# A hybrid encoder layer on one core: first transfers reordered, products of ones ahead, and a row of scales broadcast by way of DRAM

## The chip, the core and the metric

The kernel runs on one core of one Trainium2 chip. The metric is the device time of one execution in microseconds (us): a median of 3 runs, 2376.36 us (2375.31 to 2376.83) before the change. The engines are PE (matrix products; PEld is its loading of the fixed operand), DVE, ACT and POOL (elementwise work), and SP, which here does nothing but issue transfers (DMAs). Each engine runs its own list of instructions strictly in the order in which they were written, and waits on semaphores for the others.

## What is computed

One encoder layer over two sequences: a prompt of 512 tokens and a sample of 1024 tokens, width 1024. Cut to what matters here:

```python
def rms_norm(x, w):
    return x * lax.rsqrt(jnp.mean(x * x, axis=-1, keepdims=True) + NORM_EPS) * w

def hybrid_layer(x, w_in, ...):
    h = rms_norm(x, n_pre_mix)
    proj = h @ w_in
    qkv_g, z_g, a_g, b_g, q_h, f_h, i_h, g_h, gate_raw = jnp.split(proj, IN_SPLITS, axis=-1)
    ...   # Gated DeltaNet over chunks, both directions: 4 heads
    ...   # HGRN2 over chunks, both directions: 4 heads, with values i_h
    merged = gates[:, :, 0] * y_a + gates[:, :, 1] * y_b
    x = x + rms_norm(merged @ w_out, n_post_mix)
    ff = (jax.nn.silu(h2 @ w_gate) * (h2 @ w_up)) @ w_down      # h2 = rms_norm(x, n_pre_ffn)
    return x + rms_norm(ff, n_post_ffn)
```

The scale of a token, rsqrt(mean(x * x) + eps), is called `rstd` below. It can be applied to `h` before a product or to the product's result.

## The kernel before

**Tiles.** Tokens are cut into blocks of 512 (`TB`): block 0 is the prompt, blocks 1 and 2 the sample. The activations lie transposed: a tile has 128 channels on its partitions and 512 tokens in its row, eight such tiles (`KD`) to a block. A float32 factor of a large product is split in two, `hi` (rounded to the fast format fp32r by an ACT copy) and `lo` (what DVE finds left over), and each product becomes three: hi·hi, hi·lo, lo·hi (`mm3`). Small products stay in plain float32, and a plain float32 product of 128 columns is two rows of the profile.

**The order.** `layer` does not issue instructions. It records them on a `Tape`; `Tape.schedule` then plays the record against a table of costs, engine by engine, gives tiles their buffers, and returns one order in which `Tape.emit` (the line L650 of the profile) writes all instructions. So nearly all rows have the line L650, and they are told apart by the memories that they touch: `la_a`, `ba_a`, `da_a` hold tiles of 512 and more, `sa_a` and `sm_a` constants and small tiles, `ha_a` the split activations, `wa_a` the split weights, `ra_a` a matrix of ones in fp32r, `bank` the eight banks of PSUM. The constants `HOLD`, `MSTEP`, `TOKENS`, `NORMED`, `NEAR` steer which work the record and the scheduler put forward: `HOLD` and `MSTEP` say which gate projections of the dense stream are kept back until the inverse of a DeltaNet head has come to a certain step.

**The start.** `prelude` begins with block 0. For each of the eight channel tiles k, SP loads a tile `xt` of the prompt and a tile `wv` of the weights `w_ih` (256 KB each). `values(k)` then splits both: ACT writes `hi[k]` = xt · gain (the gain is a column of `vec`, so it needs that small transfer too), DVE the rest `lo[k]`, ACT and DVE the same for the weights (`wh`, `wl`). PE adds twelve products of 128x512 to four banks (`pv`). That is 96 products for all k. Ahead of them in the record stand the constants (`ident`, `ones`, masks, the vector `vec`, and what `constants()` and `ab_constants()` work out of them).

**Scales.** Block 0 is projected without its scale; its `rstd` row is applied to the results (`pn` in `proj`) until normalised tiles are there. For blocks 1 and 2 (`rstd_row`, lines 1107 to 1130), four tiles of x are squared and summed on ACT, and a [128, 4] tile `y` of scales comes out, one token to a partition. The row that later work needs has all 512 scales on every partition. It is made with PE: for each of the four columns DVE writes a diagonal matrix `dg`, PE multiplies ones by it, and ACT copies the bank to `row`. `normed` (DVE) multiplies each `xt` of the sample by it.

**The inverse.** For each DeltaNet head, 32x32 triangles are written to DRAM (`u_sc`), read back in another layout (`iu`), inverted on POOL in 31 steps (`inverse`), written to DRAM (`w_sc`), and read as `wl`, of which DVE makes `wt`. PE multiplies by both.

Of the kernel before, what the change touches and what calls it, by code (L numbers as in the profile page):

```python
# [17 lines left out]
ALU = mybir.AluOpType  # L18
# [23 lines left out]
HOLD = ((2, 2, 1, 2), (2, 2, 2, 2))  # L42
MSTEP = (24, 28)
# [6 lines left out]
VSPLIT = 4  # L50
TRIG = 0
TOKENS, NORMED = 22.0, 30.0
# [4 lines left out]
class Op:  # L57

    __slots__ = ("idx", "eng", "meth", "args", "kw", "occ", "dur", "tiles", "need", "succ", "rel", "prio", "form", "unit",
# [104 lines left out]
class Tape:  # L164
# [10 lines left out]
    NEAR = 400  # L175
# [18 lines left out]
    def __init__(self, nc):  # L194
# [11 lines left out]
        self.shift = 0  # L206

# [5 lines left out]
    @contextmanager  # L213
    def sooner(self, n):

        self.shift += n
        yield
        self.shift -= n

# [138 lines left out]
    def add(self, eng, meth, args, kw):  # L358
# [3 lines left out]
        o.eng, o.meth, o.args, o.kw = eng, meth, args, kw  # L362
        o.form, o.unit, o.port, o.part = None, [o], 0, self.part
# [72 lines left out]
    def schedule(self):  # L436
# [4 lines left out]
        for o in ops:  # L441
            o.succ = []
            o.rel = 0.0
            o.asked = False
# [321 lines left out]
def layer(ctx, tc, x_p, x_s, w_out, n_post_mix, n_post_ffn, w_down, vec, xt_p, xt_s, w_in, w_br, w_gate, w_up,  # L766
# [121 lines left out]

    ident = ctile([P, P], "ident")
# [3 lines left out]
    nc.vector.memset(ones, 1.0)  # L893
    ones_r = nc.tile(rpool, [P, P], F32R, "ones_r")
# [15 lines left out]
    vcol = ctile([P, NVEC], "vcol")  # L910
    dma(vcol, vec)
# [27 lines left out]
    def px():  # L939
        return pl.tile(psx, [P, TB], F32, "px", "px", 5)  # L940
# [166 lines left out]
    def rstd_row(blk_):  # L1107
# [14 lines left out]
        pb = px()  # L1122
        for t in range(4):
            dg = sblk("dg")
            ts(dg, ident, y[:, t:t + 1], ALU.mult)
            mm(t4(pb)[:, t, :], ones, dg)
        row = blk("row")
        copy(row, pb)
# [3 lines left out]
    rstd = {}  # L1132
    waiting = []
# [21 lines left out]
    def prelude(q):  # L1155
# [9 lines left out]
        if q.si == 0:  # L1165
            xt = []
            hi, lo = h_tiles()
            pv = [px() for t in range(4)]
            wr = []
            for k in range(KD):  # L1170
                xt.append(load(0, k))
                wr.append(blk("wv"))
                dma(wr[k], w_ih[k])
# [19 lines left out]
            constants()  # L1193
            ab_constants()
# [6 lines left out]
            for k in range(KD):  # L1201
                act(sq[k], xt[k], AF.Square)
# [1455 lines left out]
```

## Time and profile before

| what | value |
|---|---|
| median of 3 runs | 2376.36 us |
| the profiled execution, its own time | 2376.19 us |
| its span, first to last instruction | 2374.5 us |
| time outside the span | 1.7 us |
| first product on PE | 7.55 us into the span |
| end of the last product on PE | 2367.2 us |
| products on PE (rows of the profile) | 14168 |

A page of the profile has busy times by engine, the chain of work that ended last (followed back from the end, at each step to what released it) and groups of equal instructions. The timeline lists instructions as start, duration, engine, line, operation, output <- input, form, count, and in brackets the idle time of the engine before them with what ended it. Rows of equal neighbours are merged: start of the first to end of the last. "SPq" is the issuing of a transfer on SP.

### The profile page before, as it was taken

The numbers are of one execution on the slowest core, as the hardware profiler recorded it, in microseconds if no ns is written. First come the engines' busy times: TensorE is split into PE (matmuls) and PEld (weight loads), VectorE is DVE, ScalarE is ACT, GpSimd is POOL, SyncE is SP. The second block draws the span as 40 slices with busy tenths as digits, with TensorE's granted clock in tenths as the row PEclk, the third lists the DMA queues.
The fourth block names the chain that finished last, engine by engine and source line by source line (L and its number), as shares of the span: only waits on it lengthen the run. The fifth ranks groups of instructions, "written<-read, shape, count | busy, mean of one in ns | idle before, by whom it ended". The sixth has DMA issues, their size and how long they took to land.

```text
span 2374.5 us, 37882 instructions
## 1 busy us (share of the span) xinstructions
PE 2359.3 (99%) x14168; PEld 1974.5 (83%) x14168; DVE 1722.2 (73%) x2826; ACT 1244.3 (52%) x2159; POOL 753.7 (32%) x1019
## 2 busy tenths in 40 slices
PE   8999999999999999999999999999999999999998
PEld 7888888888888888888888888888888888888887
DVE  6798789858848968759856885656787887544566
ACT  6766766746637647538442464545344444433343
POOL 0534524331602612502400011124676665200221
PEclk9999999999999999999999999999999999999999
DMA  6542343221320311325874463452455544674463
GB/s 224 173 134 87 123 134 92 94 81 45 108 77 23 112 67 54 100 75 173 281 258 157 159 212 118 152 173 77 167 192 177 178 159 173 217 244 138 148 205 128
DMA packets 194071, 337.72 MB, mean 142 GB/s; under 512 B 53248, under 2 KB 93024, under 8 KB 193888
## 3 DMA queue, kind: packets, MB, share of 16 engines
q1 hardware_dynamic: 193888, 335.31, 42.4%
q8 instruction: 111, 1.82, 0.3%
q14 instruction: 72, 0.59, 0.1%
HBM read 254.59 MB, written 80.66 MB: 141 GB/s over the span
## 4 chain that ended last, share of the span: by engine, by line
PE 98%; DVE 1%; ACT 0%; issue 0%; POOL 0%; DVEq 0%; POOLq 0%
PE bank L650 98%; DVE la_a L650 1%; DVE ba_a L650 0%; DVE wa_a L650 0%; ACT la_a L650 0%; ACT wa_a L650 0%; DVE da_a L650 0%; DVE sm_a L650 0%; POOL sm_a L650 0%; DVE sa_a L650 0%; POOL la_a L650 0%; ACT ba_a L650 0%; DVEq L2653 0%; ACT ha_a L650 0%; POOL sa_a L650 0%
## 5 line engine op out<-in xcount | busy, mean ns | idle before, releaser
L650 PE MATMUL bank<-ha_a,wa_a 128*128 128x512 f32 x5328 | 1278.7, 394 | 0.0
L650 PEld LDWEIGHTS bank<-ha_a,wa_a 128*128 128x128 f32 x5328 | 985.1, 188 | 196.5 <-issue 1.3
L650 PE MATMUL bank<-xr_a 128*128 128x512 f32 x1386 | 314.3, 389 | 0.0
L650 POOL TENSOR_TENSOR ba_a<-ba_a 128x512 f32<-128x512 f32 (+1 forms) x121 | 164.2, 1361 | 453.7 <-DVE sa_a L650 211.2
L650 PEld LDWEIGHTS bank<-xr_a 128*128 128x128 f32 x1386 | 260.3, 188 | 53.8
L650 PE MATMUL bank<-xr_a,ha_a 128*128 128x512 f32 x1200 | 275.3, 389 | 0.0
L650 PEld LDWEIGHTS bank<-xr_a,ha_a 128*128 128x128 f32 x1200 | 225.4, 188 | 46.6
L650 ACT ACTIVATE la_a<-la_a 128x512 f32<-128x512 f32 (+1 forms) x324 | 204.9, 647 | 56.8 <-DVE la_a L650 42.5
L650 DVE TENSOR_TENSOR wa_a<-ba_a,wa_a 128x1024 fp32r<-128x1024 f32 (+1 forms) x109 | 128.3, 1180 | 117.2 <-PE bank L650 76.4
L650 DVE TENSOR_TENSOR wa_a<-la_a,wa_a 128x1024 fp32r<-128x1024 f32 (+1 forms) x119 | 138.1, 1164 | 70.3 <-PE bank L650 41.0
L650 ACT ACTIVATE wa_a<-ba_a 128x1024 fp32r<-128x1024 f32 (+1 forms) x109 | 105.5, 969 | 154.3 <-PE bank L650 133.5
L650 ACT ACTIVATE wa_a<-la_a 128x1024 fp32r<-128x1024 f32 (+1 forms) x119 | 115.4, 974 | 127.8 <-PE bank L650 120.0
L650 ACT ACTIVATE ha_a<-ba_a 128x512 fp32r<-128x512 f32 (+1 forms) x124 | 79.7, 645 | 151.1 <-PE bank L650 115.3
L650 PE MATMUL bank<-wa_a,ha_a 128*128 128x512 f32 x624 | 144.2, 393 | 7.5 <-ACT wa_a L650 7.5
L650 DVE TENSOR_TENSOR la_a<-la_a 128x512 f32<-128x512 f32 (+2 forms) x200 | 138.4, 705 | 12.2 <-ACT la_a L650 11.5
L650 PEld LDWEIGHTS bank<-wa_a,ha_a 128*128 128x128 f32 x624 | 118.5, 190 | 32.2 <-ACT wa_a L650 7.5
L650 DVE TENSOR_TENSOR ha_a<-ba_a,ha_a 128x512 fp32r<-128x512 f32 (+1 forms) x124 | 125.9, 1021 | 13.9 <-ACT ha_a L650 13.7
L650 DVE TENSOR_TENSOR xr_a<-da_a,xr_a 128x1024 fp32r<-128x1024 f32 (+2 forms) x60 | 71.1, 1199 | 64.1 <-ACT xr_a L650 44.0
L650 POOL TENSOR_TENSOR la_a<-la_a 128x256 f32<-128x256 f32 (+1 forms) x63 | 62.8, 1011 | 172.2 <-DVE la_a L650 79.4
L650 ACT ACTIVATE xr_a<-da_a 128x1024 fp32r<-128x1024 f32 (+2 forms) x60 | 58.5, 987 | 106.2 <-PE bank L650 105.9
L650 PE MATMUL bank<-ha_a 128*128 128x512 f32 x480 | 112.1, 389 | 0.0
L650 PEld LDWEIGHTS bank<-ha_a 128*128 128x128 f32 x480 | 90.2, 188 | 18.6
(209 smaller groups left out, 3312.5 us busy)
## 6 DMA issues: line engine op xcount, KB each, us to landing
la_a<-lay_w_in SPq DMA_DIRECT2D x62, 512.0 KB
ba_a<-lay_w_in SPq DMA_DIRECT2D x38, 512.0 KB
ba_a<-lay_w_gate SPq DMA_DIRECT2D x35, 512.0 KB
ba_a<-lay_w_up SPq DMA_DIRECT2D x34, 512.0 KB
dram_a_sc<-xa_a SPq DMA_DIRECT2D x55, 256.0 KB
ba_a<-w_ffn_down SPq DMA_DIRECT2D x23, 512.0 KB
da_a<-dram_a_sc SPq DMA_DIRECT2D x22, 512.0 KB
ba_a<-dram_a_sc SPq DMA_DIRECT2D x20, 512.0 KB
```

The costliest lines, as they stand in the source:

```text
L650: f(*[m(a) for a in o.args], **{k: m(a) for k, a in o.kw.items()})
```

## The change

The first weight tile and the first tile of the prompt become the first two transfers of SP (`w0`, `x0`); `vec` is issued by ACT. Nine products of `ones` with itself open PE's list; nothing reads their result. For k = 0, the weights are split before the activations, the activations in two halves of 256 tokens, and the twelve products go in two groups of six, tokens 0 to 255 first. The constants and the squares of block 0 carry an earliest time in the scheduler's table (`later`, `LATER`). In `rstd_row`, the four diagonals, the four products and the copy give way to two transfers: `y` to DRAM (512 elements of 4 bytes), and from there one row of 2 KB to each of the 128 partitions. The steering constants get other values.

```diff
-HOLD = ((2, 2, 1, 2), (2, 2, 2, 2))
-MSTEP = (24, 28)
+HOLD = ((1, 2, 1, 1), (2, 2, 3, 2))
+MSTEP = (22, 26)
+LATER = 9000.0
-TOKENS, NORMED = 22.0, 30.0
+TOKENS, NORMED = 14, 50
...
-    NEAR = 400
+    NEAR = 250
...
+    @contextmanager
+    def later(self, t):
+
+        old, self.after = self.after, t
+        yield
+        self.after = old
...
+        o.after = self.after
...
-            o.rel = 0.0
+            o.rel = o.after
...
+    w0 = pl.tile(tp, [P, TB + 4], F32, "wv", "t", TBUFS)[:, 0:TB]
+    dma(w0, w_ih[0])
+    vcol = ctile([P, NVEC], "vcol")
+    dma(vcol, vec, nc.scalar)
+    x0 = pl.tile(gp, [P, TB], F32, "xt", "xt", 8)
+    halves = [slice(z * 2 * P, (z + 1) * 2 * P) for z in range(2)]
+    dma(x0, xt_p[0:P, 0:TB])
...
+    warm = pl.tile(psx, [P, TB], F32, "px", "px", 5)
+    for t in range(9):
+        mm(warm[:, 0:P], ones, ones)
...
-    vcol = ctile([P, NVEC], "vcol")
-    dma(vcol, vec)
...
-        pb = px()
-        for t in range(4):
-            dg = sblk("dg")
-            ts(dg, ident, y[:, t:t + 1], ALU.mult)
-            mm(t4(pb)[:, t, :], ones, dg)
+        sc = r_sc[blk_ - 1]
+        dma(sc.rearrange("t p -> p t"), y)
         row = blk("row")
-        copy(row, pb)
+        dma(row, bass.AP(tensor=sc.tensor, offset=sc.offset, ap=[[0, P], [1, TB]]))
         rstd[blk_] = row
...
             def values(k):
-                act(hi[:, k, :], xt[k], AF.Copy, scale=g_mix[:, k:k + 1])
                 hl = pl.tile(wsp, [P, 1024], F32R, "whl", "whl", 6)
                 wh, wl = hl[:, 0:TB], hl[:, TB:2 * TB]
-                split(wh, wl, wr[k])
-                stt(lo[:, k, :], xt[k], g_mix[:, k:k + 1], hi[:, k, :].bitcast(F32), ALU.mult, ALU.subtract)
-                for x, w in ((hi, wh), (hi, wl), (lo, wh)):
-                    for t in range(4):
-                        mm(pv[t], x[:, k, t * P:(t + 1) * P], w, k == 0 and w is wh and x is hi, k == KD - 1 and x is lo)
+                if k == 0:
+                    split(wh, wl, wr[k])
+                for z in halves if k == 0 else [slice(0, TB)]:
+                    act(hi[:, k, z], xt[k][:, z], AF.Copy, scale=g_mix[:, k:k + 1])
+                if k:
+                    split(wh, wl, wr[k])
+                for z in halves if k == 0 else [slice(0, TB)]:
+                    stt(lo[:, k, z], xt[k][:, z], g_mix[:, k:k + 1], hi[:, k, z].bitcast(F32), ALU.mult, ALU.subtract)
+                for ts_ in ((0, 1), (2, 3)) if k == 0 else (range(4),):
+                    for x, w in ((hi, wh), (hi, wl), (lo, wh)):
+                        for t in ts_:
+                            mm(pv[t], x[:, k, t * P:(t + 1) * P], w, k == 0 and w is wh and x is hi, k == KD - 1 and x is lo)
...
-            constants()
-            ab_constants()
+            with nc.later(LATER):
+                constants()
+                ab_constants()
...
-            for k in range(KD):
-                act(sq[k], xt[k], AF.Square)
+            with nc.later(LATER):
+                for k in range(KD):
+                    act(sq[k], xt[k], AF.Square)
```

What this does to the lists of the engines is shown at three places. A row is a line of the kernel, an operation, output <- inputs and the output's shape; the kernel after has other line numbers (L660 for L650). Equal neighbours are merged.

The first is the start of ACT's list, before: the table load, small constants from `ident` and `vec`, then `hi` of k = 0 (ha_a), a square (la_a), the weights (wa_a).

```order
L768 ACT_TABLE_LOAD
L650 ACTIVATE sm_a,sa_a<-sa_a 128x16
L650 ACTIVATE sm_a,sa_a<-sa_a 128x32
L650 ACTIVATE sa_a<-sa_a 128x1
L650 ACTIVATE sa_a<-sa_a 128x8
L650 ACTIVATE ha_a<-la_a,sa_a 128x512
L650 ACTIVATE la_a<-la_a 128x512
L650 ACTIVATE wa_a<-la_a 128x512
```

The same place after the change:

```order
L778 ACT_TABLE_LOAD
L660 DMA sa_a<-lay_vec 128x88
L660 ACTIVATE wa_a<-la_a 128x512
L660 ACTIVATE ha_a<-la_a,sa_a 128x256 x2
L660 ACTIVATE ha_a<-la_a,sa_a 128x512
L660 ACTIVATE wa_a<-la_a 128x512
L660 ACTIVATE ha_a<-la_a,sa_a 128x512
L660 ACTIVATE wa_a<-la_a 128x512
L660 ACTIVATE sa_a<-sa_a 128x1
```

The four small constants and the square stood ahead of the first weights; now the transfer of `vec` does, and the constants come after three pairs of splits.

The second place is the start of PE's list, before: banks 87 to 90 in turn, the four token groups of `pv`.

```order
L650 MATMUL bank_87<-wa_a,ha_a 128x512
L650 MATMUL bank_88<-wa_a,ha_a 128x512
L650 MATMUL bank_89<-wa_a,ha_a 128x512
L650 MATMUL bank_90<-wa_a,ha_a 128x512
L650 MATMUL bank_87<-wa_a,ha_a 128x512
```

And after, with `pv` in banks 88 to 91:

```order
L660 MATMUL bank_87<-sm_a 128x128 x9
L660 MATMUL bank_88<-wa_a,ha_a 128x512
L660 MATMUL bank_89<-wa_a,ha_a 128x512
L660 MATMUL bank_88<-wa_a,ha_a 128x512
L660 MATMUL bank_89<-wa_a,ha_a 128x512
L660 MATMUL bank_88<-wa_a,ha_a 128x512
L660 MATMUL bank_89<-wa_a,ha_a 128x512
L660 MATMUL bank_90<-wa_a,ha_a 128x512
```

Nine products of ones stand ahead, and the first six real ones need only the first half of the tokens.

The third place is SP's list where the sample's `xt` tiles and the first head's triangles pass, before:

```order
L650 DMA la_a<-lay_xt_sample 128x512 x5
L650 DMA ba_a<-lay_xt_sample 128x512 x3
L650 DMA dram_u_sc_116<-la_a 32x4x32 x8
L650 DMA ba_a<-dram_u_sc_116 32x1024 x4
L650 DMA ba_a<-lay_w_in 128x1024
```

And after, with the two transfers of the scales of block 1 (`r_sc`):

```order
L660 DMA la_a<-lay_xt_sample 128x512 x4
L660 DMA la_a<-lay_w_in 128x1024
L660 DMA la_a<-lay_xt_sample 128x512 x4
L660 DMA dram_r_sc_106<-sm_a 128x4x1
L660 DMA ba_a<-dram_r_sc_106 128x512
L660 DMA dram_u_sc_122<-la_a 32x4x32 x4
L660 DMA dram_u_sc_122<-ba_a 32x4x32 x4
L660 DMA ba_a<-dram_u_sc_122 32x1024 x4
```

The two transfers stand ahead of the eight stores of the triangles. Counted over the whole lists, PE has 11,839 products and transposes before and 11,840 after (nine more, eight fewer), DVE has four instructions fewer and ACT one ACTIVATE or COPY fewer. PE's list changes from 128x512 products to another shape and back 243 times before and 237 times after. The last 3,474 products and transposes of PE, from about 1580 us on, stand in the same order in both.

More of the change, by code (lines that the diff above doesn't have):

```diff
@@ L57 @@
 class Op:
-    __slots__ = ("idx", "eng", "meth", "args", "kw", "occ", "dur", "tiles", "need", "succ", "rel", "prio", "form", "unit",
+    __slots__ = ("idx", "eng", "meth", "args", "kw", "occ", "dur", "tiles", "need", "succ", "rel", "after", "prio", "form", "unit",
                  "asked", "port", "part")
@@ L206, in __init__ @@
         self.shift = 0
+        self.after = 0.0
     def apart(self, pairs=False):
@@ L1132, in layer @@
     rstd = {}
+    r_sc = [dram.tile([4, P], F32, name="r_sc%d" % i) for i in range(2)]
     waiting = []
@@ L1165, in prelude @@
         if q.si == 0:
-            xt = []
+            xt = [x0]
             hi, lo = h_tiles()
             pv = [px() for t in range(4)]
-            wr = []
+            wr = [w0]
             for k in range(KD):
-                xt.append(load(0, k))
-                wr.append(blk("wv"))
-                dma(wr[k], w_ih[k])
+                if k:
+                    xt.append(load(0, k))
+                    wr.append(blk("wv"))
+                    dma(wr[k], w_ih[k])
                 if k in AHEAD:
@@ L1180, in values @@
             def values(k):
-                act(hi[:, k, :], xt[k], AF.Copy, scale=g_mix[:, k:k + 1])
                 hl = pl.tile(wsp, [P, 1024], F32R, "whl", "whl", 6)
                 wh, wl = hl[:, 0:TB], hl[:, TB:2 * TB]
-                split(wh, wl, wr[k])
-                stt(lo[:, k, :], xt[k], g_mix[:, k:k + 1], hi[:, k, :].bitcast(F32), ALU.mult, ALU.subtract)
-                for x, w in ((hi, wh), (hi, wl), (lo, wh)):
-                    for t in range(4):
-                        mm(pv[t], x[:, k, t * P:(t + 1) * P], w, k == 0 and w is wh and x is hi, k == KD - 1 and x is lo)
+                if k == 0:
+                    split(wh, wl, wr[k])
+                for z in halves if k == 0 else [slice(0, TB)]:
+                    act(hi[:, k, z], xt[k][:, z], AF.Copy, scale=g_mix[:, k:k + 1])
+                if k:
+                    split(wh, wl, wr[k])
[5 more added lines that the diff above has]
+                            mm(pv[t], x[:, k, t * P:(t + 1) * P], w, k == 0 and w is wh and x is hi, k == KD - 1 and x is lo)
             for k in range(VSPLIT):
```

## The prediction

> **What bounds the kernel now.** First the page: busy time by engine, and the chain that ended last.
>
> ```profile
> PE 2359.3 (99%) x14168; PEld 1974.5 (83%) x14168; DVE 1722.2 (73%) x2826; ACT 1244.3 (52%) x2159; POOL 753.7 (32%) x1019
> PE 98%; DVE 1%; ACT 0%; issue 0%; POOL 0%; DVEq 0%; POOLq 0%
> ```
>
> PE is 99% busy and 98% of the chain. A busy PE need not be a fast one, so I asked for its waits next: all of them, over the whole span.
>
> ```profile
> PE bank L650 <- ACT wa_a L650: 7.5, 1, 7.5
> PE bank L650 <- DVE wa_a L650: 0.2, 1, 0.2
> ```
>
> PE waits 7.5 us once, for the first split weights, and 0.2 us later. From then on the time is the sum of PE's products and of what lies behind the last one. So three things can shorten it: an earlier first product, faster products, fewer products. The chain in order of time shows what the first product waits for:
>
> ```profile
> 5.21 0.32 DVE sm_a L650 x2
> ...
> 7.55 145.17 PE bank L650 x941
> ```
>
> Not a transfer: the chain comes from DVE's masks. The timeline shows what lies between, and the transfers.
>
> ```profile
> 0.80 1.28 ACT L768 ACT_TABLE_LOAD   x1 [0.80 <-PEq L2648]
> 0.80 0.39 SPq L650 DMA_DIRECT2D sa_a<-lay_vec  x1
> 0.90 0.17 DVE L650 MEMSET sm_a<- 128x128 f32 x1 [0.90 <-PEq L2648]
> 1.24 0.42 SPq L650 DMA_DIRECT2D la_a<-lay_xt_prompt  x1
> 1.71 0.43 SPq L650 DMA_DIRECT2D la_a<-lay_w_ih  x1
> 2.09 0.21 ACT L650 ACTIVATE sm_a<-sa_a 128x16 f32<-128x16 f32 x1
> 2.65 0.43 SPq L650 DMA_DIRECT2D la_a<-lay_w_ih  x1
> 2.72 0.20 ACT L650 ACTIVATE sa_a<-sa_a 128x1 f32<-128x1 f32 x1
> 5.63 0.21 ACT L650 ACTIVATE sa_a<-sa_a 128x8 f32<-128x8 f32 x1 [2.71 <-DVE sa_a L650]
> 5.75 0.71 ACT L650 ACTIVATE ha_a<-la_a,sa_a 128x512 fp32r<-128x512 f32 x1
> 6.36 0.61 ACT L650 ACTIVATE la_a<-la_a 128x512 f32<-128x512 f32 x1
> 6.88 0.61 ACT L650 ACTIVATE wa_a<-la_a 128x512 fp32r<-128x512 f32 x1
> 7.32 0.33 SPq L650 DMA_DIRECT2D la_a<-lay_w_ih  x1
> ```
>
> ACT stands idle for 2.71 us behind DVE; then `hi`, a square and the weights follow in a row, and PE starts.
>
> **Term 1, the first product.** When are `w0` and `x0` there? The transfer view of two windows, 0 to 4.0 us and 0 to 4.8 us:
>
> ```profile
> DMA packets 384, 0.50 MB, mean 125 GB/s; under 512 B 161, under 2 KB 161, under 8 KB 384
> DMA packets 518, 0.75 MB, mean 155 GB/s; under 512 B 176, under 2 KB 176, under 8 KB 518
> ```
>
> 0.50 MB had moved at 4.0 us and 0.75 MB at 4.8 us. `vec` and the first two tiles are 0.57 MB, so the pair was through at about 4.2 us, and at the latest near 4.8. Without `vec` ahead of it the pair's second is issued 0.47 us earlier (1.24 for 1.71): both there between 3.75 and 4.35 us, the first of them some 0.65 us (256 KB at that pace) before. I take 3.7 for `w0` and 4.35 for `x0`. ACT splits `w0` in 0.61 us, to 4.3. `vec` is the open piece: ACT issues it, behind its table load in the list. It goes out at 0.80 if the load doesn't hold the list up, at 2.08 if it does; before, it was read at 2.72, at most 1.92 us after its issue. That makes 2.7 to 4.0 us, in time either way; I take the later. At the worst it takes what the fifth tile took, issued at 2.65, whose landing let the thirteenth transfer go at 7.32 (the transfers use eight semaphores in turn): 4.7 us, so 6.8. Half of `hi` is 0.71 us less half of what 512 more columns cost in this row:
>
> ```profile
> 41.92 1.07 ACT L650 ACTIVATE wa_a<-la_a 128x1024 fp32r<-128x1024 f32 x1 [0.45 <-PE bank L650]
> ```
>
> (1.07 - 0.61) / 2 = 0.23, so 0.48 us. PE starts at 4.35 + 0.48 + 0.06 (the step from 7.49 to 7.55 above) = **4.9 us** instead of 7.55: **-2.65 us**, bounds 4.3 and 7.3. After that k = 1 needs the fifth tile's counterpart, issued 0.47 us earlier and so there at 6.85, split by 7.5; k = 0 keeps PE until 4.9 + 12 x 0.227 = 7.6. No wait there. The constants and squares that are moved behind cost ACT and DVE the same time later; these rows show the cover:
>
> ```profile
> 10.00:20.00 10.00, 10.00 (x42) 8.20 (x41) 6.39 (x11) 10.00 (x18) 0.14 (x2) 1.00 1.03 399
> 20.00:30.00 10.00, 10.00 (x46) 8.29 (x45) 4.32 (x5) 3.10 (x4) 0.00 (x0) 1.00 1.03 415
> ```
>
> (busy PE, PEld, DVE, ACT, POOL, then clock and transfers). ACT is full from 10 to 20 us and then idle for two thirds. In 23 us, from 3.7 to 26.7, it has 8 x (0.71 + 0.61 + 0.61) and four weight splits of 1.07, 20 us: it fits, with 3 us to spare. Without the cover each k would wait some tenths. A page of the Trainium skill speaks against this term: "ScalarE: Activation LUTs", What ACT_TABLE_LOAD costs, has 2.66 us for a load with its drain. By that `vec` would go out at 3.46, land at 5.4, and PE start at 5.9, 1.0 us later than I say. The trace disagrees: ACT's next instruction ran at 2.09, right behind the 1.28 us of the load.
>
> **Term 2, the pace of the first products.** The same products in two stretches, and the granted clock (the 1.00 before the last two numbers) in the first of them; last the group that most products are in (count, busy us, mean ns of one):
>
> ```profile
> 7.55 4.77 PE L650 MATMUL bank<-wa_a,ha_a 128*128 128x512 f32 x11 [7.55 <-ACT wa_a L650]
> 7.55 24.04 PE L650 MATMUL bank<-wa_a,ha_a 128*128 128x512 f32 x96 [7.55 <-ACT wa_a L650]
> 8.00:9.00 1.00, 1.00 (x4) 1.00 1.01 375
> L650 PE MATMUL bank<-ha_a,wa_a 128*128 128x512 f32 x5328 | 1278.7, 394 | 0.0
> ```
>
> The other 85 took 24.04 - 4.77 = 19.27 us, 0.227 each. The eleven took about 0.42 each, though the clock column says 1.00: PE begins at half pace, for some 4.2 us. That costs 11 x 0.227 = 2.5 us against 4.6 (4.77 less the 0.16 by which a product's row, 0.39, outlasts its step): 2.1 us. After the change `ones` is there at 1.07 (DVE's first row above), the nine products start at about 1.1, and PE is busy until 4.9 if they run at half pace: 2 rows x 0.111 (below) x 0.42 / 0.227 = 0.41 each, 3.7 in all. If what frees the pace is 4.2 us of busy time, it comes at 5.3, and one real product pays 0.2. So **-1.9 us**, bounds 0 and -2.1. "TensorE: Matmul & The Clock Gate", Part 1, in the Trainium skill has a rule by which it could be less: the pace doubles after a busy window of 3.4 us that runs free of the kernel, so 3.4 to 6.8 us of work may pass. By that the real products would run slow until 4.5 to 7.9 us and the term would be -2.1 to -0.6; the 4.2 us here lie inside.
>
> **Term 3, the products that go.** The four products of block 1 in PE's list, and what comes before and after:
>
> ```profile
> 77.08 0.17 DVE L650 TENSOR_TENSOR sm_a<-sm_a 128x4 f32<-128x4 f32 x1
> 77.28 0.87 DVE L650 TENSOR_SCALAR sm_a<-sa_a,sm_a 128x128 f32<-128x128 f32 x4
> 89.00 1.06 PE L650 MATMUL bank<-sm_a 128*128 128x128 f32 x8
> 89.81 1.41 PE L650 MATMUL bank<-ha_a,wa_a 128*128 128x512 f32 x5
> 106.92 2.10 DVE L650 SCALAR_TENSOR_TENSOR la_a<-la_a,sa_a 128x512 f32<-128x512 f32 x3
> ```
>
> Eight rows in 0.8 to 0.9 us, 0.111 each. Two blocks: 16 x 0.111 = **-1.8 us**. In their place SP writes and reads 512 numbers: the scale is there at 77.25 and first used at 106.92, almost 30 us later. The slowest stand-in, the eight stores and the read further down, takes 10.2 us from the first store to POOL's use (71.08 to 81.25), so PE doesn't see it; without the cover it would cost up to that. DVE's and ACT's part (0.87 and a copy per block) lay beside PE and gives nothing. The order has six changes of shape fewer; a return to 128x512 costs (1.41 - 0.39 - 4 x 0.227) = 0.11 us and the last small product before it 0.08 less, so 0.2 us in all: left out.
>
> **Sum.** 2.65 + 1.9 + 1.8 = 6.35 us off the execution's own 2376.19 (span 2374.5 plus 1.7): **2369.8**. The median of the runs shown is 0.17 above that execution, which I neglect.
>
> **Rivals.** (A) The products of ones free nothing, or late, and the real ones run at half pace as before: up to 2369.8 + 1.9 = 2371.7. For it: the clock column shows nothing of what holds the pace down. The Trainium skill's free window would end between 2369.6 and 2371.1. Chance 0.10. (B) `vec` is late, held up by more of ACT's list than the 1.28 us or between SP's big tiles, and PE starts between 5.9 and 7.3: 2370.8 to 2372.2. The Trainium skill's drain is the mild end of it. Against: it landed within 1.92 us before. 0.08. (C) The new order waits more. Before, PE waited 0.2 us after the start, but with DVE near full:
>
> ```profile
> 100.00:150.00 50.00, 50.00 (x405) 40.72 (x404) 44.90 (x92) 31.97 (x54) 24.01 (x50) 1.00 0.33 101
> 150.00:200.00 50.00, 49.90 (x380) 42.32 (x379) 46.66 (x82) 40.45 (x75) 29.00 (x58) 1.00 0.36 130
> ```
>
> DVE is idle for 8.4 of these 100 us (44.90 and 46.66 busy). Three more `pn` evictions come in, eight diagonals go, about even; but a block done early only gains what DVE can follow. If half of terms 1 and 2 is lost there or in small waits, 2372 to 2374.5. 0.15. (D) Slower: SP stands still. The read of the scales waits for the store's 512 pieces of 4 bytes, and behind it in SP's list are the stores of the first head's triangles, behind those POOL's inverse, behind that PE.
>
> ```profile
> 71.08 4.16 SPq L650 DMA_DIRECT2D dram_u_sc<-la_a  x8
> 76.58 1.98 SPq L650 DMA_DIRECT2D ba_a<-dram_u_sc  x4
> 81.25 0.42 POOL L650 TENSOR_TENSOR sm_a<-la_a,ba_a 128x31 f32<-128x31 f32 x1 [23.36 <-DMA ba_a<-dram_u_sc]
> 126.98 0.21 PE L650 MATMUL bank<-ba_a,la_a 32*32 32x32 f32 x1
> ```
>
> PE's first use of the inverse is its 588th product before; in the new order 620 real ones come ahead of it, some 33 x 0.227 = 7.5 us of work more. It decides from a hold-up of 7.5 us on. The eight stores, 1024 pieces, took 5.5 us to the read, so I expect 2 to 5. To be slower than 2381 it would take 7.5 + 6.35 + 4.75 = 18.6 us: price 5 us and more over before, time about 2382. 0.05. And the rest, 0.02, better than the bounds of the three terms.
>
> **How the numbers follow.** 0.2% is 4.75 us, about what can be told from no change here: faster means under 2371.6, slower over 2381.1. Forecast 0.60 (2368 to 2371.5), A 0.10, B 0.08, C 0.15, D 0.05, rest 0.02. Faster: 0.60, the rest, half of A and B: 0.71. Slower: D, 0.05. Same: 0.24. The range goes from 2367.8 (PE at 4.3, no slow product, six cheaper changes) to 2373.8, which takes in A, B and most of C.
>
> **What would show it.** Right: the 96 products of `pv` begin near 4.9 us, at 0.227 from the first or second on, and end near 26.8 instead of 31.6; PE's list of waits has one of under 1 us after that; DVE's first use of the scale lies well behind the read. Wrong: a wait of PE for `ha_a` at the start (B), products of 0.42 after 5.5 us (A), new waits for DVE's tiles between 40 and 200 us (C), or for `wl`'s (D).

## The result, and the profile after

| kernel | median | runs | ratio to before (95%) |
|---|---|---|---|
| before | 2376.77 us | 11 | 1 |
| after | 2382.78 us | 11 | 1.0026 [1.0017, 1.0035] |

The change makes the kernel slower by 0.26%, 6.2 us of 2376.4; faster by 6.6 us was forecast, in a range that ends at 2373.8. The profiled execution after took 2383.97 us. First its page: busy time by engine, and the chain by engine.

```profile
PE 2365.3 (99%) x14170; PEld 1976.6 (83%) x14170; DVE 1727.2 (73%) x2822; ACT 1246.9 (52%) x2158; POOL 757.3 (32%) x1019
PE 90%; DVE 5%; DMA 2%; ACT 1%; issue 1%; POOL 0%; SPq 0%; DVEq 0%; POOLq 0%; ACTq 0%
```

PE reads 99% busy as before, yet it is 90% of the chain instead of 98%, and transfers are 2% of it. PE's busy time even rose by 6.0 us; the products of ones are 3.9 of them, and yet it has fewer real products than before, so some of these ran longer. So next PE's waits, then the start of the timeline.

```profile
PE bank L660 <- DVE ba_a L660: 3.3, 3, 1.9
PE bank L660 <- DVE wa_a L660: 1.6, 3, 1.2
PE bank L660 <- issue: 1.2, 1, 1.2
PE bank L660 <- DVE sm_a L660: 1.1, 1, 1.1
PE bank L660 <- ACT wa_a L660: 1.1, 2, 0.6
PE bank L660 <- DVE la_a L660: 1.0, 1, 1.0
```

```profile
0.83 0.39 ACTq L660 DMA_DIRECT2D sa_a<-lay_vec  x1
1.12 3.93 PE L660 MATMUL bank<-sm_a 128*128 128x128 f32 x18 [1.12 <-DVE sm_a L660]
3.81 0.63 ACT L660 ACTIVATE wa_a<-la_a 128x512 fp32r<-128x512 f32 x1 [1.73 <-DMA la_a<-lay_w_ih]
4.51 1.52 ACT L660 ACTIVATE ha_a<-la_a,sa_a 128x256 fp32r<-128x256 f32 x3
5.07 22.06 PE L660 MATMUL bank<-wa_a,ha_a 128*128 128x512 f32 x96
```

The start came out as worked out: `w0` read at 3.81 (3.7 forecast), `x0` at 4.51 (4.35), the first real product at 5.07 (4.9), and 96 products in 22.06 us, 0.228 each from the first on. They end at 27.1 instead of 31.6, 4.5 us earlier. The list of waits has what that was lost to: apart from the 1.1 us for `ones`, about 8 us of new ones, 7 of them for results of DVE and ACT. What comes late there, the chain in order of time tells (pieces between 60 and 140 us):

```profile
66.51 8.24 DMA dram_r_sc<-sm_a
74.77 5.04 DMA ba_a<-dram_r_sc
...
84.00 3.83 DMA ba_a<-x_sample
...
95.71 0.70 DVE ba_a L660
...
96.46 2.58 PE bank L660 x8
...
102.78 8.40 DMA dram_r_sc<-sm_a
```

and SP's part of the timeline what stood behind it:

```profile
66.51 0.38 SPq L660 DMA_DIRECT2D dram_r_sc<-sm_a  x1
74.77 0.33 SPq L660 DMA_DIRECT2D ba_a<-dram_r_sc  x1
75.20 1.81 SPq L660 DMA_DIRECT2D dram_u_sc<-la_a  x4
...
82.25 1.71 SPq L660 DMA_DIRECT2D ba_a<-dram_u_sc  x4
84.00 0.42 SPq L660 DMA_DIRECT2D ba_a<-x_sample  x1
```

The store of 512 pieces of 4 bytes lands 8.2 us after its issue. SP stands before the read until then, and all behind it is late: the triangles, and a tile of `x_sample`. ACT squares that tile, is late with what follows in its list, DVE with it, and PE waits 1.9 us at 94.6. There is a second price. The view by windows shows busy time by engine, the granted clock (the number before the last two), then transfers:

```profile
95.00:96.00 1.00, 0.00 (x0) 0.00 (x0) 0.29 (x1) 1.00 (x3) 0.77 (x4) 1.00 0.99 395
96.00:97.00 1.00, 0.54 (x5) 0.54 (x5) 0.40 (x1) 1.00 (x2) 0.87 (x2) 0.89 0.84 330
97.00:98.00 1.00, 1.00 (x5) 0.81 (x4) 0.65 (x1) 1.00 (x3) 0.81 (x3) 0.50 0.51 186
98.00:99.00 1.00, 1.00 (x4) 0.81 (x3) 0.41 (x2) 0.28 (x2) 0.76 (x4) 0.50 0.62 125
99.00:100.00 1.00, 1.00 (x4) 0.81 (x3) 1.00 (x2) 0.94 (x1) 1.00 (x1) 0.50 0.99 375
100.00:101.00 1.00, 1.00 (x5) 0.78 (x5) 0.19 (x1) 1.00 (x4) 0.80 (x3) 0.90 0.27 107
```

Behind the wait the clock is halved for 3.4 us (0.11, three times 0.50 and 0.10 short of full, over 0.50), and PE counts as fully busy meanwhile. That costs up to 1.7 us and stands in no list of waits. It happens twice more, near 138 and 319 us (0.79 in the mean of 134 to 142, 0.76 of 316 to 323). Together this is an account of the loss, as an estimate: 8.2 us of new waits and three times 1.7 us of pace, less the 4.5 us of the start and 1.2 to 1.8 us for the products that went, make 7.0 to 7.6 us; the two profiled executions differ by 7.8 (2383.97 and 2376.19).

### The profile page after: what moved, and what is told of

Same layout as the page of the kernel before. It is cut to its first block, busy times and chain, and to the rows that moved or that the text cites. A ratio compares the mean times of both kernels' runs of the same rounds, so it can differ in the third digit from the quotient of the medians.

```text
span 2382.2 us, 37911 instructions
## 1 busy us (share of the span) xinstructions
PE 2365.3 (99%) x14170; PEld 1976.6 (83%) x14170; DVE 1727.2 (73%) x2822; ACT 1246.9 (52%) x2158; POOL 757.3 (32%) x1019
## 4 chain that ended last, share of the span: by engine, by line
PE 90%; DVE 5%; DMA 2%; ACT 1%; issue 1%; POOL 0%; SPq 0%; DVEq 0%; POOLq 0%; ACTq 0%
PE bank L660 90%; DVE la_a L660 3%; DVE ba_a L660 1%; DMA dram_r_sc<-sm_a 1%; ACT la_a L660 1%; DMA ba_a<-x_sample 1%; DVE wa_a L660 0%; DMA la_a<-lay_w_in 0%; DVE sm_a L660 0%; ACT ba_a L660 0%; SPq L660 0%; ACT wa_a L660 0%; POOL la_a L660 0%; DMA ba_a<-dram_r_sc 0%; DMA dram_g_sc<-la_a 0%
## 5 line engine op out<-in xcount | busy, mean ns | idle before, releaser
L660 PE MATMUL bank<-ha_a,wa_a 128*128 128x512 f32 x5328 | 1283.7, 395 | 2.1 <-DVE wa_a L660 1.6
L660 PEld LDWEIGHTS bank<-ha_a,wa_a 128*128 128x128 f32 x5328 | 986.9, 189 | 201.4 <-DVE wa_a L660 2.8
L660 PE MATMUL bank<-xr_a 128*128 128x512 f32 x1386 | 314.3, 389 | 0.0
L660 PEld LDWEIGHTS bank<-xr_a 128*128 128x128 f32 x1386 | 260.1, 188 | 54.0
L660 POOL TENSOR_TENSOR ba_a<-ba_a 128x512 f32<-128x512 f32 (+1 forms) x135 | 184.6, 1372 | 287.3 <-DVE ba_a L660 85.9
L660 PE MATMUL bank<-xr_a,ha_a 128*128 128x512 f32 x1200 | 275.2, 389 | 0.0
L660 PEld LDWEIGHTS bank<-xr_a,ha_a 128*128 128x128 f32 x1200 | 225.2, 188 | 46.8
L660 ACT ACTIVATE la_a<-la_a 128x512 f32<-128x512 f32 (+1 forms) x298 | 188.3, 649 | 52.1 <-DVE la_a L660 28.7
L660 DVE TENSOR_TENSOR wa_a<-ba_a,wa_a 128x1024 fp32r<-128x1024 f32 (+1 forms) x113 | 132.5, 1174 | 108.3 <-PE bank L660 54.6
L660 ACT ACTIVATE wa_a<-ba_a 128x1024 fp32r<-128x1024 f32 (+1 forms) x113 | 109.3, 968 | 164.5 <-PE bank L660 157.5
L660 DVE TENSOR_TENSOR wa_a<-la_a,wa_a 128x1024 fp32r<-128x1024 f32 (+1 forms) x115 | 134.0, 1166 | 55.7 <-PE bank L660 40.8
L660 ACT ACTIVATE wa_a<-la_a 128x1024 fp32r<-128x1024 f32 (+1 forms) x115 | 112.0, 976 | 108.9 <-PE bank L660 90.4
L660 ACT ACTIVATE ha_a<-ba_a 128x512 fp32r<-128x512 f32 (+1 forms) x126 | 80.4, 645 | 153.6 <-PE bank L660 114.3
L660 PE MATMUL bank<-wa_a,ha_a 128*128 128x512 f32 x624 | 142.2, 389 | 0.0
L660 DVE TENSOR_TENSOR la_a<-la_a 128x512 f32<-128x512 f32 (+2 forms) x205 | 132.2, 663 | 12.3 <-ACT la_a L660 10.2
L660 PEld LDWEIGHTS bank<-wa_a,ha_a 128*128 128x128 f32 x624 | 117.0, 188 | 24.4 <-ACT ha_a L660 0.2
L660 DVE TENSOR_TENSOR ha_a<-ba_a,ha_a 128x512 fp32r<-128x512 f32 (+1 forms) x126 | 125.9, 1007 | 12.6 <-ACT ha_a L660 12.6
L660 POOL TENSOR_TENSOR la_a<-la_a 128x256 f32<-128x256 f32 (+2 forms) x69 | 69.0, 1016 | 192.4 <-ACT la_a L660 79.6
L660 DVE TENSOR_TENSOR xr_a<-da_a,xr_a 128x1024 fp32r<-128x1024 f32 (+2 forms) x60 | 71.1, 1199 | 64.1 <-ACT xr_a L660 44.0
L660 ACT ACTIVATE xr_a<-da_a 128x1024 fp32r<-128x1024 f32 (+2 forms) x60 | 58.5, 987 | 106.0 <-PE bank L660 105.7
L660 PE MATMUL bank<-ha_a 128*128 128x512 f32 x480 | 112.0, 389 | 0.0
L660 ACT ACTIVATE ba_a<-ba_a 128x512 f32<-128x512 f32 (+1 forms) x153 | 98.3, 651 | 17.1 <-DVE ba_a L660 7.7
```

Of the source, the lines that this page charges most:

```text
L660: f(*[m(a) for a in o.args], **{k: m(a) for k, a in o.kw.items()})
```

## The experiments

Four theories on where the time went were open. **1**: SP's stand-still behind the store. **2**: the order that the scheduler made anew, from the changed record and the new steering constants. **3**: the start's gain is real, and stays as long as the order behind it stays. **4**: it isn't, since a PE that starts earlier only meets the other engines late. 5 (each edit is worth what was forecast; the landing of the store and the new order took it away) and 6 (the two transfers disturb SP in any order, or the eight products go without a gain) came later. All ratios are to the kernel before on the same chip.

| kernel | median us | ratio to before (95%) |
|---|---|---|
| e1_read_late | 2379.63 | 1.0014 [1.0005, 1.0023] |
| e6_priced | 2379.32 | 1.0013 [1.0004, 1.0022] |
| s1_store128 | 2377.34 | 1.0007 [0.9998, 1.0016] |
| e4_dram_row | 2386.38 | 1.0042 [1.0029, 1.0054] |
| f1_row128 | 2377.20 | 1.0004 [0.9995, 1.0013] |
| e3_start_only | 2379.03 | 1.0015 [1.0006, 1.0024] |
| h1_warm_by_hand | 2375.80 | 0.9998 [0.9989, 1.0007] |
| h2_start_by_hand | 2372.08 | 0.9984 [0.9975, 0.9993] |
| b1_all_by_hand | 2372.91 | 0.9985 [0.9976, 0.9993] |
| b2_store_behind | 2371.31 | 0.9980 [0.9971, 0.9988] |
| d1_pe_later | 2388.50 | 1.0053 [1.0041, 1.0066] |
| e5_old_const | 2389.30 | 1.0052 [1.0039, 1.0064] |
| c1_new_const | 2384.53 | 1.0033 [1.0020, 1.0045] |
| e2_pe_row | 2381.35 | 1.0021 [1.0013, 1.0030] |
| g1_fill | 2383.83 | 1.0028 [1.0018, 1.0038] |

Differences of 1 us lie within these intervals. But kernels with the same list on PE can be compared product by product: each product has its place in the list, and its start can be set against that of the same product in the other trace. This shows where a difference arises. Minus is earlier (us):

| same product, at | 32 us | 100 us | 150 us | 400 us | 1000 us | 2000 us |
|---|---|---|---|---|---|---|
| h1_warm_by_hand against before | -1.96 | -1.63 | -1.49 | -1.23 | -1.11 | -0.38 |
| h2_start_by_hand against before | -4.30 | -4.30 | -3.91 | -4.03 | -3.91 | -4.42 |
| b1_all_by_hand against before | -3.66 | -2.84 | -3.26 | -2.86 | -2.85 | -3.40 |
| b2_store_behind against before | -3.32 | -4.23 | -4.55 | -4.59 | -4.17 | -4.67 |
| e1_read_late against after | 0.41 | -3.07 | -4.06 | -2.76 | -2.72 | -2.81 |
| e6_priced against after | -0.09 | -3.82 | -4.31 | -3.80 | -3.08 | -3.18 |
| s1_store128 against after | -0.16 | -4.12 | -6.49 | -7.54 | -6.75 | -6.88 |
| d1_pe_later against after | 3.19 | 2.40 | -0.63 | -0.23 | 4.60 | 4.56 |
| g1_fill against after | 0.42 | -1.28 | -3.01 | -1.86 | -0.08 | -0.10 |
| f1_row128 against e4_dram_row | 0.14 | 0.06 | -9.30 | -9.94 | -10.13 | -10.36 |

### The store: read later, price, pieces

**e1_read_late** moves one instruction of SP after the order is made:

```diff
     order = nc.schedule()
...
+    order = put_off(order, "r_sc0", 17)   # the read of r_sc0, 17 places later among SP's
```

> The changed kernel with its order untouched on every engine but SP: there the read of the first block's scales stands 17 places later in the list, behind the stores and reads of the first head's triangles and four tiles of x_sample. Theory 1 (SP stands still for the 8.2 us in which the store of 512 pieces lands, and what is queued behind it comes late): the waits of PE at 94 us (1.9) and at 135 us (0.5 and 1.2) and the stretches at half pace behind them (1.6 us each) go, so about 2376 us, 6.8 less than the 2382.8 of the changed kernel. Theory 2 (the new order and the new steering constants cause the waits): PE's list is the same, so the waits stay and the time is 2382 to 2383.

**e6_priced** changes the scheduler's table:

```diff
             if vo is None or vo.pool.kind == "DRAM":
-                o.dur = 1200.0
+                o.dur = 7200.0 if run == 1 else 1200.0
```

> The changed kernel with one number of the scheduler's cost table changed: a store to DRAM in pieces of one element is priced at 7.2 us and its pieces instead of 1.2 us and its pieces. The lists of PE, DVE, ACT and POOL come out as in the changed kernel, the read of the first scales comes behind the eight stores of the triangles, that of the second one place later. Theory 1: as with the read moved by hand, 2376 us, within 1 us of it. Theory 2: 2382 to 2383.

2379.63 and 2379.32: 3 us better than after, half of what theory 1 gave. SP in e6_priced goes on with the triangles at 71.27 instead of 75.20 and waits 2.5 us for the store:

```profile
66.30 0.39 SPq L660 DMA_DIRECT2D dram_r_sc<-sm_a  x1
71.27 1.77 SPq L660 DMA_DIRECT2D dram_u_sc<-la_a  x4
...
75.37 0.34 SPq L660 DMA_DIRECT2D ba_a<-dram_r_sc  x1
```

The wait at 94.6 is gone with its half pace (-3.07 and -3.82 at 100 us in the comparison above), the others stay. Theory 1 is right for one wait, not for all.

**s1_store128** keeps after's order and makes the pieces larger. The scales then stand in DRAM in another order than the row needs, so this kernel's output is not the layer's; its work is the same:

```diff
-        dma(sc.rearrange("t p -> p t"), y)
+        dma(bass.AP(tensor=sc.tensor, offset=sc.offset, ap=[[4, P], [1, 4]]), y)
```

> The changed kernel with its own order, and the two stores of scales made in 128 pieces of 16 bytes instead of 512 of 4 (the scales then stand in DRAM in another order than the row needs, so the normalised activations of the sample are scaled wrongly; all work is the same). If the landing of 8.2 us hangs on the number of pieces: the store lands in about 3 us, SP goes on 5 us earlier, and the time is that of the priced kernel, 2379. If each such store lands this late whatever its pieces: as the changed kernel, 2382 to 2383.

```profile
66.03 0.33 SPq L660 DMA_DIRECT2D dram_r_sc<-sm_a  x1
67.43 0.33 SPq L660 DMA_DIRECT2D ba_a<-dram_r_sc  x1
```

128 pieces are down in 1.4 us instead of 8.2 (2.0 in the second block, 98.73 to 100.72); the landing hangs on how the 2 KB are cut. 2377.34 is 5.4 us better than after by the medians, 4.5 by the ratios. In the trace it is 6.9, since none of its waits was followed by half pace.

**e4_dram_row** puts the broadcast alone into the kernel before (the part of the change's diff with `r_sc`), **f1_row128** does so with 128 pieces, for which it loads four consecutive tokens to a partition:

```diff
-            dma(xs, x_rows(blk_ * 4 + t))
+            dma(xs, x_s[0, (blk_ - 1) * TB:blk_ * TB, :].rearrange("(p t) d -> t p d", t=4)[t])
```

> The kernel before with the broadcast of the scales by way of DRAM alone; start, steering constants and vec as before. Theory 1: SP stands still for some 8 us here too, and PE waits for it: 1.8 us less for the products and 3 to 7 us more for waits and half pace, 2378 to 2382. Theory 2: the stand-still is hidden, and only the eight products go: 2374.6.

> The kernel before with the broadcast by way of DRAM alone, in the order that it got there, but with the store in 128 pieces of 16 bytes (tokens 4p to 4p + 3 on partition p, as above). If the 8 us landing of the 512 pieces made PE's wait of 6.9 us at 131 us: that wait goes, 7 to 9 us less than 2386.4, so 2377.5 to 2379.5. If the order that was made anew made it: it stays, 2386.

SP and PE's longest wait in e4_dram_row, then SP in f1_row128:

```profile
78.62 0.39 SPq L650 DMA_DIRECT2D dram_r_sc<-sm_a  x1
...
89.88 0.34 SPq L650 DMA_DIRECT2D la_a<-dram_r_sc  x1
```

```profile
PE bank L650 <- DVE wa_a L650: 6.8, 1, 6.8
```

```profile
78.62 0.34 SPq L650 DMA_DIRECT2D dram_r_sc<-sm_a  x1
...
81.81 0.35 SPq L650 DMA_DIRECT2D la_a<-dram_r_sc  x1
```

2386.38, worse than theory 1 had it; the landing took 11.2 us here and 10.4 in the second block (105.25 to 115.7), and by the chain PE's wait of 6.8 us, up to 130.9, came of the second. With 128 pieces the wait is gone: 9.2 us by the medians, a little more than expected. With the cheap store the broadcast alone is within the measurement of before. Its eight products don't show: the order was made anew here too, and PE waits 2.0 us in it where before waited 0.2 (without the start).

### The start, and the order that is made anew

**e3_start_only** has the change's start in the kernel before, and nothing else.

> The kernel before with the new start alone (w0 and x0 first, vec issued by ACT, nine products of ones, k = 0 in halves, constants and squares later), the broadcast on PE and the old steering constants. If the start is worth what it showed in the changed kernel (the products of pv ended 4.5 us earlier): 2376.4 - 4.5 = 2371.9. If the order behind it can't follow (theory 2: DVE and ACT near full), the gain is lost in waits between 30 and 330 us: 2374 to 2378.

2379.03: the start itself is there (96 products from 5.05 in 22.06 us), and yet 7 us are lost behind it, in waits that before doesn't have. The longest are 2.2 us at 66.9, ahead of products for which after waits 1.0 us at 65.1, and 1.1 us at 554, where after has none. Theories 2 and 4 would both say so. What tells them apart is nearly the same start (without the halves of k = 0) and no new order. **h1_warm_by_hand** and **h2_start_by_hand** let the scheduler make the order of before, and change the list afterwards:

```diff
     order = nc.schedule()
...
+    order = by_hand(order, [                                      # h2 only
+        ("sync", [15, 14], None), ("scalar", [13], None),         # w0, x0; vec
+        ("scalar", [36, 35, 51, 52, 196], 125), ("scalar", [99, 103], 84),
+        ("vector", [37, 38, 54, 53], 123), ("vector", [102, 100, 104, 105, 106, 107, 108], 86)])
+    order = ahead_of_all(order, 9)                                # h1: 20 products of ones
```

> The kernel before with its own order on every engine, and only 20 products of ones put ahead of PE's list (they end near 7.3 us, where the first real product starts anyway). Theory 3 (what the start gains is a gain, as long as the order behind it stays): the first eleven real products run at 0.227 instead of 0.42, 2.0 us less, 2374.3. Theory 4 (in the kernel before PE runs some 3.7 us behind where the scheduler's table has it, and the other engines use this as a lead; who starts PE earlier meets them late): the 2.0 us come back as waits between 55 and 330 us, 2376.

> The kernel before with its own order, and only its first instructions moved by hand: w0 and x0 ahead on SP, vec issued by ACT, ACT's split of w0 and x0 ahead of the constants, nine products of ones ahead of PE's list. From about 15 us on each engine's list is that of the kernel before, word for word; the broadcast stays on PE. First real product near 5.3 us at full pace, pv ends near 27.2 instead of 31.5. Theory 3: 4.3 us less, 2372.1, with no new wait over 0.5 us. Theory 4: 2 to 4 us of new waits between 55 and 330 us, 2374.5 to 2376.4.

2372.08, what theory 3 gave (that it is so to the tenth is chance, with an interval of 2 us to each side). PE's first rows and its list of waits in h2_start_by_hand:

```profile
1.12 3.92 PE L650 MATMUL bank<-sm_a 128*128 128x128 f32 x18 [1.12 <-DVE sm_a L650]
5.20 22.09 PE L650 MATMUL bank<-wa_a,ha_a 128*128 128x512 f32 x96 [0.16 <-ACT ha_a L650]
```

```profile
PE bank L650 <- DVE sm_a L650: 1.1, 1, 1.1
PE bank L650 <- ACT ha_a L650: 0.2, 1, 0.2
```

No wait behind the start, and the 4.3 us of 32 us are still 4.4 at 2000 us. h1_warm_by_hand gains 1.96 us at the start, as theory 3 has it, and keeps 0.4 of it; 0.3 go at 65 us and 1.3 near 1117, where PE stood 1.1 us for nothing that the profile shows. Its time alone would have spoken for theory 4.

**d1_pe_later** tries theory 4 from the other end: e6_priced with sixteen more products of ones ahead.

> The kernel with the store priced at 7.2 us, and sixteen more products of ones ahead of PE's list: they keep PE until about 8.4 us, so its real work starts 3.4 us later than in that kernel (4.97) and about as late as in the kernel before. Nothing else is moved. Theory 4: its waits (8.5 us in 12 places) shrink by what PE starts later, and the time stays at 2379 to 2380. If the waits are made by the order alone and hang on PE's own work: they stay, and the time is 2379.3 + 3.4 = 2382.7.

2388.50: 9.2 us more than e6_priced for a start 3.3 us later. The waits did not shrink; their sum grew, from 7.1 to 11.4 us with the 1.1 for `ones`:

```profile
PE bank L660 <- issue: 2.9, 1, 2.9
PE bank L660 <- DVE la_a L660: 2.5, 1, 2.5
```

Theory 4 falls: of the 3.3 us, 3.0 are in sum still there at 400 us, product by product against e6_priced. Another 4.6 come in one place, with the 2.9 us under "issue" (at 424 us) and the half pace behind them; where those 2.9 us come from, the profile doesn't show, and it stays open. Why the waits didn't shrink isn't shown either; that a late PE also delays the engines that it feeds would explain it.

**e5_old_const** is after with before's HOLD, MSTEP, NEAR, TOKENS and NORMED; **c1_new_const** is before with the new ones; **e2_pe_row** is after with the broadcast back on PE.

> The changed kernel with the steering constants of before (HOLD, MSTEP, NEAR, TOKENS, NORMED). If the new constants brought the waits that are left without the stand-still of SP (65, 132, 254, 314, 817, 1003 us, some 6 us): 2377. If they were chosen for the new record and the old ones fit it worse: 2384 to 2388.

> The kernel before with the new steering constants alone. If the constants bring waits by themselves: 2379 to 2383, with waits of PE at other places than in the changed kernel. If they are harmless: 2376.

> The changed kernel with the broadcast of the scales back on PE; start and steering constants as changed, the order made anew. Without the 8 us store 6.9 us go (as with 128 pieces), eight products come back, 1.8: 2377.7 if the remade order is as good; the scheduler's own table puts its last product 3.8 us later than in the changed kernel, so up to 2381.5. With a time under 2374 the new order would not be to blame for what is left.

2389.30, 2384.53 and 2381.35, the first two 1.3 and 1.5 us beyond what was expected of a bad fit, the third at its upper end. The constants are not the fault of after by themselves: the old ones are worse still with the new record, and the new ones are worse with the old record, by 7.8 us (0.33%), with PE's waits at 246, 263 and 426 us instead. Undoing the broadcast alone gives back 1.4 us of 6, which lies within the intervals. Record and constants fit as a pair, and each of the orders made anew here waits more than before's; which waits come is not to be read from the parts.

### All three edits in the order of before

**b1_all_by_hand** adds the broadcast to h2_start_by_hand in the same way (the constants stay as in before, and k = 0 whole): diagonals, products and copies taken out of the list, a store of 128 pieces right behind the instruction that makes the scales, the read where the copy stood. **b2_store_behind** differs in one place of SP's list:

```diff
-        order.insert(spot(a - 1) + 1, transfer(sc, y))
+        order.insert(spot(1089 if i == 0 else a - 1) + 1, transfer(sc, y))   # 1089: the last x_sample tile
```

> The kernel before with its own order and the start moved by hand, and the broadcast by way of DRAM put into that order by hand: the diagonals, their products and the copies are taken out, SP stores the scales right behind the instruction that makes them and reads the row where the copy stood. The four tiles of x that give the scales of a block are loaded with tokens 4p to 4p + 3 on partition p, so that the store is 128 pieces of 16 bytes and stands in the order that the row needs. Theory 5 (each edit is worth what was forecast, and what went wrong is the 8 us store and the order that was made anew): 2372.1 - 1.8 = 2370.3. Theory 6 (the transfers disturb SP in any order, or the eight products go without a gain): 2372 to 2375.

> As the kernel with all three edits put into the order of before by hand, but the store of the first block's scales stands nine places later in SP's list, behind the four reads of the triangles and the tiles of x_sample that it held up by 2.1 us there (SP waited for the scales). Theory 5: the wait of PE at 90 us (1.7) is gone, and the eight products come out: 2372.1 - 1.8 = 2370.3. Theory 6 (they go without a gain whatever SP does): 2372 to 2373.

In b1_all_by_hand the store of the scales stood ahead of the reads of the triangles and made them wait for the scales, to 74.93; with no store there (h2_start_by_hand) and behind (b2_store_behind), they go at 72.77 and 74.24:

```profile
74.36 0.34 SPq L650 DMA_DIRECT2D r_sc<-sm_a  x1
74.93 1.96 SPq L650 DMA_DIRECT2D ba_a<-dram_u_sc  x4
```

(b1_all_by_hand; below b2_store_behind)

```profile
74.24 1.71 SPq L650 DMA_DIRECT2D ba_a<-dram_u_sc  x4
...
80.29 0.50 SPq L650 DMA_DIRECT2D r_sc<-sm_a  x1
```

The first costs a wait of 1.5 us at 88.3 that eats the four products just gained. The second doesn't have it: against before its products gain 0.9 us more between 32 and 100 us, and 0.3 more by 150 (-3.32, -4.23, -4.55), while those of h2_start_by_hand stay at -4.30 and then lose 0.4. At 32 us it is 1.0 us behind h2_start_by_hand only because part of its first products ran at half pace in this execution. 2371.31 us, 0.20% [0.12%, 0.29%] less than before, is the lowest time of all kernels here, below before and below after, which is 0.26% over before. Its difference to h2_start_by_hand lies within the intervals. It is 1.0 us above the 2370.3 expected.

### The half pace behind a wait

**g1_fill** fills the wait at 94.6 in after:

```diff
     order = nc.schedule()
+    k = next(i for i, o in enumerate(order) if o.idx == 827)   # the transpose that waits
...
+    order = order[:k] + fill + order[k:]                       # 8 products of ones, same bank
```

> The changed kernel with its own order, and eight products of ones put into PE's wait of 1.9 us at 94.5 to 96.4 us (into the bank that the next transpose writes anyway; eight at 0.22 us are 1.8 us). If it is standing still that halves the pace afterwards: the products behind run at 0.227 instead of 0.427, 1.5 us less, 2381.3, and the granted clock has no 0.5 at 97 us. If the half pace comes from the small products there or from elsewhere: the 0.5 at 97 us stays, 2382.8.

```profile
94.78 1.95 PE L660 MATMUL bank<-sm_a 128*128 128x128 f32 x16
```

```profile
97.00:98.00 1.00, 1.00 (x8) 0.87 (x7) 0.60 (x1) 1.00 (x3) 0.79 (x3) 1.00 0.87 268
98.00:99.00 1.00, 1.00 (x6) 0.83 (x5) 0.99 (x2) 1.00 (x3) 0.89 (x2) 1.00 0.79 154
```

The clock is 1.00 at 97 to 99 us and the products behind are 1.7 us earlier (from 0.42 to -1.28): standing still is what halves the pace, and the counts in the last section bear this out over all traces. The time, 2383.83, is not better: other waits at 358 and 422 us take it back (-1.86 at 400 us, -0.08 at 1000). As an improvement it fails.

## Why the prediction was wrong

**What bounds the kernel.** "From then on the time is the sum of PE's products": true of before's list, and taken over for a list that did not exist yet. This is the step that failed most. The sum was made from parts that are nearly right one by one, but the change makes the scheduler write a new order, and no term stood for that; only rival C did, bounded by half of terms 1 and 2. The ladder, in us against before by the ratios (times 2376.4):

| kernel | against before | step |
|---|---|---|
| start, in before's order (h2_start_by_hand) | -3.8 | -3.8 |
| and the broadcast, in before's order (b2_store_behind) | -4.8 | -1.0 |
| all parts, new constants, order made anew, store of 128 pieces (s1_store128) | +1.7 | +6.4 |
| after: store of 512 pieces | +6.2 | +4.5 |

Each step has an uncertainty of some 3 us from the intervals. The first, the third and the fourth are clear of that. The second is not; there only the comparison by products speaks for a gain. The third joins the record, the constants and the order made of them; c1_new_const and e5_old_const show that these don't add up one by one.

**Terms 1 and 2, the start: right, term 2 with luck.** 5.07 for 4.9, at 0.228 from the first product on; 4.5 us in sum forecast and 4.5 measured at the end of `pv` in after, 4.3 in h2_start_by_hand. The transfer of `vec` went out at 0.83, beside the table load. So the drain that the Trainium skill has in "ScalarE: Activation LUTs", What ACT_TABLE_LOAD costs, did not delay it; rivals A and B did not come. The 4.2 us after which PE was to run at full pace are no fixed price, though. The clock record of a trace begins with the change to full pace (ahead of it, at half pace, the view by windows has no record and shows 1.00): 11.84 us in before, 4.3 us after PE's first product, and 4.62 us in after, 3.5 us after it. In e3_start_only it came after 2.8 us, in b2_store_behind after 6.2, and its real products ran slow until 7.3 us and lost 1.0. So A's "late" does come, in other executions. Two slips in the working changed nothing: 256 KB at the pace of the two transfer views (0.25 MB in 0.8 us) take 0.84 us instead of 0.65, but `x0` decides; and the parts named for the low end of the range give 2368.8, not 2367.8.

**Term 3, fewer products: right in kind, over-sized, and its cover wrong.** The count is as forecast (14170 rows with eighteen of ones). In before's order the eight products give 1.2 us at most by products (b2_store_behind) instead of 1.8. The step that failed is "The eight stores, 1024 pieces, took 5.5 us to the read, so I expect 2 to 5": SP stood still for 8.0 us in each block. The stand-in was eight stores of 128 pieces of 128 bytes, and the number of pieces in all was taken as the measure; one store of 512 pieces of 4 bytes is another thing. Whether the number in one store or their size makes it, no run separates. The "almost 30 us" of cover for the scales themselves was right, and beside the point: what was late was the work queued behind.

**Rival D: the right mechanism, with a price and a path that were wrong.** SP stood still, and it was given 0.05 because it would need 18.6 us to become slower by itself. That count went by one path, the triangles and the inverse, with its 7.5 us of cover. The tile of `x_sample` stood in the same list and had less: it reached PE by way of ACT and DVE at 94.6. And a wait was priced at its own length, where 1.9 us cost 3.6 with the half pace behind it (-0.20 to -3.82 in e6_priced between 94 and 100 us).

**Rival C: the right mechanism, half the size.** "If half of terms 1 and 2 is lost there or in small waits, 2372 to 2374.5"; the new order took 6.4 us, more than the start gives. It was bounded by the gain, as if a new order could only fail to use it. By the ratios c1_new_const loses 7.8 us against before, and e3_start_only 7.4 and e2_pe_row 8.8 against h2_start_by_hand, which has nearly the same start in before's order: a new order cost 7 to 9 us in these three. It need not: f1_row128, made anew for the broadcast alone, ends 1.0 us over before where 1.2 to 1.8 less were due. Which property of before's order keeps it free of waits isn't settled; theory 4, a lead of the other engines, was tried and fell.

**What was said to show it** did: new waits for DVE's tiles (C), waits behind SP (D), none for `ha_a` over 0.5 us (B), no products of 0.42 after 5.5 us at the start (A).

## What to carry to other kernels

Where a scheduler writes the order, an edit is two changes: the edit, and a new order for everything behind it; measure the edit in the old order first (here by moving a few instructions in the finished list), and take the order up apart from it. Before a transfer is put into a queue that others use, ask what its landing holds up, and shape it by contiguous pieces: which token lands on which partition is free, and 512 pieces of 4 bytes became 128 of 16 that way (f1_row128, b2_store_behind). A wait of a full engine can cost its length and as much again in pace, which the list of waits does not show; the granted clock by windows does.

## What the runs showed of the hardware

A store of 512 pieces of 4 bytes to DRAM landed after 8.2 and 8.4 us (after), 11.2 and 10.4 (e4_dram_row); the same 2 KB in 128 pieces of 16 bytes after 1.4 and 2.0 us (s1_store128). The Trainium skill, "DMA: Bandwidth & Descriptors", Rules for kernel authors, says that a non-contiguous last dimension becomes one descriptor per element and should be rearranged; the runs agree, and give the price. The moving of the pieces is not it: in after all 512 had gone by 67.8 us, from 68 to 74.7 us no DMA moved anything, and the landing came at 74.8. What it waits for no view shows.

The pace halves for 3.4 us behind waits that are shorter than that: 1.9 us at 94.6, 1.2 us at 317 in after. "TensorE: Matmul & The Clock Gate", Why this matters for your kernels, in the Trainium skill warns of gaps over some 3 us; the measurement decides here. Nor does length alone decide. The wait of 1.2 us at 312 to 319 us is in six kernels with the same list on PE. It was followed by half pace in four (after, e1_read_late, e6_priced, g1_fill) and not in two (s1_store128, d1_pe_later). The clock in windows over it, e6_priced and s1_store128:

```profile
312.00:320.00 8.00, 6.80 (x50) 5.23 (x50) 6.23 (x11) 4.03 (x9) 1.69 (x6) 0.79 0.45 159
```

```profile
310.00:318.00 8.00, 6.80 (x59) 5.62 (x60) 7.78 (x15) 4.44 (x10) 1.46 (x6) 1.00 0.48 161
```

The same page of the Trainium skill, Part 1, has a window of 3.4 us that runs free of the kernel. The clock records agree: in each of the 17 traces every change of the clock lies on a grid of steps of 3.413 us, to within 0.004 us, and each trace's grid starts elsewhere. In after the clock falls at 96.78, 137.74 and 318.64 us, 12 and 53 steps apart, and each half pace is one step long. Two of its three falls, the step ahead and the step at half pace:

```profile
93.37:96.78 3.41, 1.53 (x9) 0.99 (x8) 0.69 (x1) 3.41 (x7) 2.78 (x9) 1.00 1.01 383
96.78:100.19 3.41, 3.41 (x12) 2.74 (x10) 2.25 (x3) 2.63 (x6) 2.91 (x7) 0.50 0.71 236
315.23:318.64 3.41, 2.20 (x23) 1.19 (x23) 3.30 (x7) 3.08 (x6) 1.73 (x6) 1.00 0.00 0
318.64:322.06 3.42, 3.42 (x22) 2.82 (x23) 3.27 (x6) 1.02 (x2) 0.53 (x1) 0.50 0.71 234
```

So what counts is what PE does within one step. From the change to full pace to the last product, over the 17 traces, PE stood 1.88 us or longer in nine steps, and each was followed by half pace. It stood 1.20 to 1.73 us in fifteen, of which six were, and under 1.20 us none was. In d1_pe_later the wait of 1.2 us lies across two steps (0.69 and 0.52 us); in s1_store128 it lies in one, and the pace stayed. An estimate made afterwards fits better: count 0.227 us for each product of 512 columns that starts in the step, and a smaller one by its columns and its share of 128x128. Then the four have 0.65 to 0.89 us of work in that step, s1_store128 1.25 and d1_pe_later 1.48. Over all steps at full pace the two groups overlap only between 1.03 and 1.16 us. No run was made to test this.
